# Block 0's attention chain in hand order, its heads four at a time

## The chip, the cores and the metric

The kernel runs on one core of a Trainium2 chip. The metric is device time in microseconds. The engines named below are PE (TensorE, matmuls and transposes), DVE (VectorE), ACT (ScalarE), POOL (GpSimd, which here issues the gathers) and SP (SyncE, which issues most loads). Lines such as L262 are lines of the kernel before; the order listings of the change have lines of the changed file, some 5 to 100 higher.

## The reference, cut

A decoder layer over 512 tokens of width 1024, float32: an attention layer with two groups of eight heads of 64, one output projection, a normalization, then a retrieval layer over 16384 single-neuron experts, and a second normalization.

```python
def hybrid_mixer(x, w_in, w_out):
    proj = x @ w_in                       # six groups of 512 columns
    qa, ka, va, qb, kb, vb = jnp.split(proj, cuts, axis=-1)
    qa = partial_rotary(split_heads(qa, DIL_HEADS), pos)
    ka = partial_rotary(split_heads(ka, DIL_HEADS), pos)
    oa = dilated_window_attention(qa, ka, split_heads(va, DIL_HEADS))
    ob = stick_breaking_attention(...)
    return concatenate([oa, ob]) @ w_out

x = layer_norm(ALPHA * x + mix)
# peer: scores of x @ w_query against sub_keys, top 16 of each half,
# 16 of the sums, softmax gates, then for 128 chosen experts per token
#   h = x . u[e];  y = sum gate * gelu(h) * v[e]
x = layer_norm(ALPHA * x + peer(x))
```

A heads are softmax attention with a mask that holds logarithms of multiplicities; B heads weigh by exponentials of sums of log-sigmoid terms, which the kernel makes with a triangular matmul.

## The kernel before

The 512 tokens are four blocks of 128. Block 0 goes alone and first, in plain float32 (a matmul of two records on PE): its six projection groups, its A heads, its B heads, output projection, normalization, queries of the retrieval, routing. Only then is it known which experts its tokens want, and POOL can start to gather rows of `peer_u` (L739, 128 rows of 4 KB each). Everything for blocks 1 to 3 (projection in split form with three matmuls a product, `mm3`, L127 to L129; A heads; B heads) is laid beside the gathers of blocks 0 and 1. Blocks 2 and 3 go through all experts in dense form later.

The steps of block 0:

- `project_block0` (L244) yields 24 times, four weight loads of 512 KB per group, into four buffers in turn (`WBUF` = 4), each freed by its matmuls (L262). The groups follow `GROUPS` (L225): keys A, values A, queries A, keys B, values B, queries B. `place_tok` (L234) scales the result on ACT (L239), rotates it on DVE (L214 to L217, "rot" groups), and `turn` (L219) transposes it on PE (L222) and copies it on ACT (L223).
- `head_a` (L311) and `head_b` (L334) do one head each. A: scores (L315), mask and minimum on DVE (L318), exponential with sum on ACT (L321), transpose (L325), copy (L328), values (L331). B: scores and mask (L339, L341), three ACT operations (L345 to L347), one on DVE (L349), the triangular matmul (L351), an exponential (L355), values (L359). `close_a`, `close_b` (L362, L368) finish eight heads; `place` (L390) transposes them into `o0f`.
- `project_first` (L467): output projection by column halves, c = 0 over all eight slices of weight rows, then c = 1; `add_out` (L455) adds the residual and takes statistics.
- `normalize` (L503), with its transposes on PE (L173) and copies on ACT (L527) back into `x0f`; then `query_first` (L558) with its matmuls at L568 and L572.
- `load_x2` (L720) loads the four 512 KB blocks of x. `project_in` (L269) is the projection of blocks 1 to 3: in its first group it also loads eight pieces `xt` of 192 KB and splits them on ACT (L207) and DVE (L208); its weights are split at L120 and L124.

Up to here the steps are given as generators, taken in turns (`run`, with a ratio for each), and a scheduler orders the instructions of each engine from them. From the B heads of blocks 1 to 3 on (`tc.manual_schedule`, L929) the order is as written. Each engine and each DMA queue works in its order; SP's queue is one of them.

```python
    run(pb, attend_a(0), load_x2(), (3, 2, 1))
    run(attend_b(0))
    run(project_first())
    norm = normalize(0)
    next(norm)
    run(head(proj, 3))
    run(norm)
    first = query_first()
```

Of the kernel before, what the change touches and what calls it, by code (L numbers as in the profile page):

```python
# [92 lines left out]
def build(ctx, nc, tc, a):  # L93
# [131 lines left out]
    GROUPS = ("rot", kA, 1.0), ("tok", 0, 1.0), ("rot", qA, -0.125), ("t", kB, 1.0), ("tok", 512, 1.0), ("t", qB, 0.125)  # L225
# [7 lines left out]

    def place_tok(tb, kind, dst, scale, ps):  # L234
        if kind == "tok":
            nc.scalar.activation(v[:, tb, dst:dst + 512], ps, AF.Copy)
            return
        q = qw.tile([P, NH, HD], F32, name="q", bufs=2)
        nc.scalar.activation(q.rearrange("p h d -> p (h d)"), ps, AF.Copy, scale=scale)  # L239
        if kind == "rot":  # L240
            rotary(q, tb)
        turn(q, dst)

    def project_block0():  # L244
        for g, (kind, _, scale) in enumerate(GROUPS):
# [3 lines left out]
            for i in range(4):  # L249
# [3 lines left out]
                if g == i == 0:  # L253
                    for k in range(2):
                        (nc.scalar, nc.sync)[k].dma_start(w[:, k], src[:, k])
                        (nc.sync, nc.scalar)[k].dma_start(x0f[:, 2 * k:2 * k + 2], a["xT"][:, 2 * k:2 * k + 2, :P])
                    nc.scalar.dma_start(x0f[:, 4:], a["xT"][:, 4:, :P])
                else:
                    nc.sync.dma_start(w, src)
                for k in range(kn):  # L260
                    kk = kn * kq + k
                    nc.tensor.matmul(ps[:, ch * wd:(ch + 1) * wd], x0f[:, kk], w[:, k], start=kk == 0, stop=kk == KD - 1)  # L262
                yield
# [3 lines left out]
            place_tok(0, kind, dst, scale, ps)  # L267

    def project_in():  # L269
        tbs = PARTS[1]  # L270
        n = len(tbs)
        for g, (kind, _, scale) in enumerate(GROUPS):
# [3 lines left out]
            for i in range(4):  # L276
# [6 lines left out]
                wh, wl = wload(a["w_in"][g, i].rearrange("p (k c) -> p k c", k=kn), [P, kn, wd])  # L283
                if kind == "t" and kq == 0:
# [120 lines left out]
    def attend_a(tb):  # L405
        done = []
        yield from heads_a(tb, done)
        place(done)

    def attend_b(tb):  # L410
        done = []
        yield from heads_b(tb, done)
        place(done)
# [53 lines left out]
    def project_first():  # L467
        for c in range(2):
            ps = bank("h")
            for kq in range(4):  # L470
                w = wraw(a["w_out"][c, kq], [P, 2, 512])
                for k in range(2):
                    kk = 2 * kq + k
                    nc.tensor.matmul(ps, o0f[:, kk], w[:, k], start=kk == 0, stop=kk == KD - 1)
                yield
            add_out(0, c, ps)
# [301 lines left out]
    run(head(pb, 12))  # L778
# [102 lines left out]

    tags = cycle("ab")
    proj = project_in()
# [360 lines left out]
```

## Time and profile before

| what | value |
|---|---|
| median of three runs | 1484.0 us (1479.2, 1484.0, 1486.96) |
| the profiled execution, its own time | 1485.58 us |
| its span, first to last instruction | 1483.7 us |
| granted TensorE clock, mean | 0.966 |
| PE busy, share of the span | 1383.8 us, 93% |
| DVE busy | 1197.7 us, 81% |
| ACT, POOL busy | 520.2 and 694.6 us |
| mean HBM rate | 334 GB/s |

The shares are means over stages with different limits. PE's busy time counts pipelined matmuls from issue to a modelled end. In the chain of work that ended last the gathers of `peer_v` and `peer_u` hold 27% of the span.

### The profile page before, as it was taken

Reading aid. Unit: us, or ns where it says so; the run is one execution under the profiler, and the core shown is the slowest. Engines: PE = TensorE matmul, PEld = TensorE weight load, DVE = VectorE, ACT = ScalarE, POOL = GpSimd, SP = SyncE. Lnnn points to the kernel's source line nnn. Section 1 sums busy time; section 2 is a strip of 40 time slices with the busy share of each in tenths; the row PEclk is TensorE's granted clock in tenths of the full one; section 3 lists DMA queues with packets and bytes.
Section 4 is the critical chain, followed back from the end, with each engine's and each line's share of the span. In section 5 each row is a group of like instructions: output and inputs, shape, how many; then the busy total and the mean of one; then the engine's idle time right before and its main releaser. Section 6 shows DMA issues by size and latency. Waiting matters only on the chain.

```text
span 1483.7 us, 19664 instructions
## 1 busy us (share of the span) xinstructions
PE 1383.8 (93%) x6654; PEld 1119.6 (75%) x6654; DVE 1197.7 (81%) x2473; ACT 520.2 (35%) x1073; POOL 694.6 (47%) x526
## 2 busy tenths in 40 slices
PE   7989889999989999588899999999999999999796
PEld 3659677677648998467678888888888888887575
DVE  0137998878888999999998778778788887888887
ACT  1422334455432111399942222222222222222352
POOL 0000478667755333203556666655556555556200
PEclk9889999999889999799999999999999999999898
DMA  8756899889969999658999999999999999999872
GB/s 290 238 175 219 285 363 330 315 319 391 323 240 401 329 310 310 223 179 285 282 357 410 410 410 409 410 409 410 409 410 410 409 409 410 409 409 405 322 248 89
DMA packets 163221, 495.95 MB, mean 334 GB/s; under 512 B 15376, under 2 KB 48288, under 8 KB 163120
## 3 DMA queue, kind: packets, MB, share of 16 engines
q0 software_dynamic: 74304, 270.13, 48.3%
q1 hardware_dynamic: 86432, 218.66, 40.2%
q10 hardware_dynamic: 2384, 5.90, 1.1%
q8 instruction: 53, 0.87, 0.2%
q14 instruction: 48, 0.39, 0.1%
HBM read 477.78 MB, written 16.84 MB: 333 GB/s over the span
## 4 chain that ended last, share of the span: by engine, by line
PE 35%; DMA 31%; DVE 23%; issue 6%; ACT 4%; POOL 1%; SPq 0%; ACTq 0%; DVEq 0%; POOLq 0%
DMA g<-peer_v,eidx 15%; DMA g<-peer_u,eidx 12%; PE y L1112 8%; PE h L856 7%; DVE x L759 3%; DVE yg L759 3%; DVE o L813 2%; PE m L262 2%; DMA v<-peer_v 2%; PE m L497 1%; POOL g L739 1%; PE tr L497 1%; PE h L359 1%; PE h L331 1%; ACT o L822 1%
## 5 line engine op out<-in xcount | busy, mean ns | idle before, releaser
L739 POOL DMA_INDIRECT g<-peer_u,eidx x256 | 356.5, 1392 | 337.9 <-DVE topi L544 146.3
L739 POOL DMA_INDIRECT g<-peer_v,eidx x256 | 332.3, 1298 | 350.2 <-DVE x L759 112.0
L856 PE MATMUL h<-xf,w 128*128 128x256 f32 x2048 | 474.0, 380 | 0.0
L856 PEld LDWEIGHTS h<-xf,w 128*128 128x128 f32 x2048 | 384.0, 191 | 52.3
L748 DVE SCALAR_TENSOR_TENSOR g<-g,x 128x1024 f32<-128x1024 f32 x256 | 305.5, 1221 | 46.2 <-DMA g<-peer_u,eidx 45.6
L1112 PE MATMUL y<-vh,a 128*128 128x512 f32 x928 | 288.7, 415 | 9.1 <-ACT a L1098 8.3
L1112 PEld LDWEIGHTS y<-vh,a 128*128 128x128 f32 x928 | 175.7, 190 | 50.1 <-ACT a L1098 10.9
L124 DVE TENSOR_TENSOR vl<-v,vh 128x1024 fp32r<-128x1024 f32 x122 | 148.9, 1221 | 44.9 <-ACT vh L1067 44.6
L759 DVE SCALAR_TENSOR_TENSOR x<-g,hg,x 128x1024 f32<-128x1024 f32 x128 | 163.8, 1280 | 23.4 <-DMA g<-peer_v,eidx 22.6
L759 DVE SCALAR_TENSOR_TENSOR yg<-g,hg,yg 128x1024 f32<-128x1024 f32 x126 | 161.4, 1281 | 25.7 <-DMA g<-peer_v,eidx 25.1
L848 ACT ACTIVATE gl<-h 128x256 f32<-128x256 f32 x128 | 48.7, 380 | 310.1 <-PE h L856 310.0
L1112 PE MATMUL y<-vl,a 128*128 128x512 f32 x464 | 147.2, 399 | 1.0 <-DVE vl L124 1.0
L1067 ACT ACTIVATE vh<-v 128x1024 fp32r<-128x1024 f32 x122 | 128.5, 1053 | 38.0 <-PE y L1112 16.2
L1112 PEld LDWEIGHTS y<-vl,a 128*128 128x128 f32 x464 | 87.8, 190 | 22.4 <-DVE vl L124 2.4
L1098 ACT ACTIVATE a<-gl 128x512 fp32r<-128x512 f32 x58 | 36.3, 627 | 167.0 <-DVE gl L1092 167.0
L822 ACT ACTIVATE o<-o1b,sg 128x128 f32<-128x128 bf16 x256 | 83.5, 400 | 3.4 <-DVE o1b L807 3.2
L262 PE MATMUL m<-w,x0f 128*128 128x256 f32 (+1 forms) x128 | 48.6, 523 | 8.6 <-DMA x0f<-xT 7.9
L828 PEld LDWEIGHTS m<-o,o 128*128 128x128 f32 x304 | 37.7, 191 | 20.9 <-ACT o L822 18.0
L828 PE MATMUL m<-o,o 128*128 128x128 f32 x304 | 41.7, 280 | 11.8 <-ACT o L822 7.1
L128 PE MATMUL m<-wl,x2h 128*128 128x512 f32 x96 | 40.3, 420 | 6.1 <-DVE wl L124 6.0
L813 DVE TENSOR_TENSOR o<-sg,c_small 128x512 f32<-128x512 f32 x64 | 43.9, 686 | 2.4 <-PE a L828 2.2
L262 PEld LDWEIGHTS m<-w,x0f 128*128 128x128 f32 x128 | 24.2, 201 | 26.0 <-issue 11.4
(256 smaller groups left out, 1865.2 us busy)
## 6 DMA issues: line engine op xcount, KB each, us to landing
w<-uT SPq DMA_DIRECT2D x128, 512.0 KB, 8.7
v<-peer_v SPq DMA_DIRECT2D x128, 512.0 KB, 7.3
w<-w_in SPq DMA_DIRECT2D x47, 512.0 KB, 5.0
gt<-gd SPq DMA_DIRECT2D x15, 960.0 KB, 11.3
w<-peer_wq SPq DMA_DIRECT2D x16, 512.0 KB, 4.3
wq<-peer_wq SPq DMA_DIRECT2D x16, 512.0 KB, 6.7
gd<-stage SPq DMA_DIRECT2D x15, 512.0 KB, 5.1
gd<-stage SPq DMA_DIRECT2D x15, 448.0 KB, 3.7
```

What stands on the lines that cost most here:

```text
L124: nc.vector.tensor_sub(parts[1], src, parts[0].bitcast(F32))
L262: nc.tensor.matmul(ps[:, ch * wd:(ch + 1) * wd], x0f[:, kk], w[:, k], start=kk == 0, stop=kk == KD - 1)
L739: nc.gpsimd.indirect_dma_start(out=u, out_offset=None, in_=a["peer_v" if kind else "peer_u"], in_offset=bass.IndirectOffsetOnAxis(ap=eidx[ ...
L748: nc.vector.scalar_tensor_tensor(u, u, 1.0, x, op0=OP.mult, op1=OP.mult, accum_out=hs[:, j:j + 1])
L759: nc.vector.scalar_tensor_tensor(acc, u, hs[:, j:j + 1], acc, op0=OP.mult, op1=OP.add)
L813: nc.vector.tensor_tensor(hot2[s], gate[tb][1][:, 0, t:t + TG, None].to_broadcast([P, TG, P]), iota[:, None, :].to_broadcast([P, TG, P]), ...
L822: nc.scalar.activation(hot[s][:, j], o1b[:, :, j], AF.Copy, scale=gate[tb][1][:, 1, t + j:t + j + 1])
L828: nc.tensor.matmul(gps[s][:, j * P:(j + 1) * P], o2[:, j], o1[:, j], start=True, stop=True)
L848: nc.scalar.activation(gls[c // 2][:, c % 2], ps[:, :ND], AF.Gelu)
L856: nc.tensor.matmul(hps[c][:, :ND], us[c][:, k], xf[:, k], start=k == 0, stop=k == KD - 1)
L1067: nc.scalar.activation(vsp[c][0], vs[c], AF.Copy)
L1112: nc.tensor.matmul(yps[t][hf], s_, w_[:, hf * 512:(hf + 1) * 512], start=c == 0 and n == 0, stop=c == P - 1 and n == len(terms) - 1)
```

## The change

It puts block 0's part, from the first 12 projection steps to the second half of normalization, into manual order, and changes how the work is cut:

- The first rows of x come as an array of their own, `x0T`, contiguous, all but one piece through SP's queue.
- Queries B are projected ahead of values B, in block 0 and in blocks 1 to 3. The turn of a group is put off by one or two projection steps (`late`).
- `four_a` and `four_b` take four heads (the even ones, or the odd) as one piece of 512 columns: one score bank, one DVE and ACT operation for each step. In `four_a` the minimum and the sum are separate DVE operations.
- `first_out(kq)` does the output projection by weight rows: slices 0 and 1 for both column halves while only the A half of `o0f` is there.
- x is loaded later; of the eight `xt` pieces two are loaded ahead of the queries instead of eight, and two projection steps of blocks 1 to 3 run there instead of three.

```diff
-    GROUPS = ("rot", kA, 1.0), ("tok", 0, 1.0), ("rot", qA, -0.125), ("t", kB, 1.0), ("tok", 512, 1.0), ("t", qB, 0.125)
+    GROUPS = ("rot", kA, 1.0), ("tok", 0, 1.0), ("rot", qA, -0.125), ("t", kB, 1.0), ("t", qB, 0.125), ("tok", 512, 1.0)
...
-                        (nc.sync, nc.scalar)[k].dma_start(x0f[:, 2 * k:2 * k + 2], a["xT"][:, 2 * k:2 * k + 2, :P])
-                    nc.scalar.dma_start(x0f[:, 4:], a["xT"][:, 4:, :P])
+                        (nc.sync, nc.scalar)[k].dma_start(x0f[:, 2 * k:2 * k + 2], a["x0T"][:, 2 * k:2 * k + 2])
+                    nc.sync.dma_start(x0f[:, 4:], a["x0T"][:, 4:])
...
+                n += 1
+                if n in late:
+                    turn(*late.pop(n))
                 yield
...
-            place_tok(0, kind, dst, scale, ps)
+            if kind == "tok":
+                place_tok(0, kind, dst, scale, ps)
+            else:
+                late[n + (2 if kind == "rot" else 1)] = scaled(0, kind, scale, ps), dst
...
                 wh, wl = wload(a["w_in"][g, i].rearrange("p (k c) -> p k c", k=kn), [P, kn, wd])
+                if g == i == 0:
+                    yield
...
+    def four_a(g, st, tag):
+        ps = bank(tag).rearrange("p (i t) -> p i t", i=4)
+        hs = slice(g, NH, 2)
+        rows = slice(g * 64, g * 64 + 64)
+        for i in range(4):
+            nc.tensor.matmul(ps[:, i], qA[0][rows, i], kA[rows, i, :P], start=True, stop=True)
+        yield
+        u, w = (work.tile([P, 512], F32, name="su", bufs=5).rearrange("p (i t) -> p i t", i=4) for _ in range(2))
+        nc.vector.tensor_add(u, ps, maska[:, None, 3 * P:].to_broadcast([P, 4, P]))
+        nc.vector.tensor_reduce(st["nm"][:, hs], u, axis=AX.X, op=OP.min)
+        nc.vector.tensor_sub(u, u, st["nm"][:, hs, None].to_broadcast([P, 4, P]))
+        nc.scalar.activation(u, u, AF.Exp, scale=-1.0)
+        nc.vector.reduce_sum(st["z"][:, hs], u, axis=AX.X)
+        yield
+        for i in range(4):
+            nc.tensor.transpose(ps[:, i], u[:, i], ident)
+        yield
+        nc.scalar.activation(w, ps, AF.Copy)
+        yield
+        for i in range(4):
+            h = 2 * i + g
+            nc.tensor.matmul(st["po"][:, h * HD:(h + 1) * HD], w[:, i], v[:, 0, h * HD:(h + 1) * HD], start=True, stop=True)
+        yield
+
+    def four_b(g, st, tag):
+        zf = bank(tag)
+        ps = zf.rearrange("p (i t) -> p i t", i=4)
+        rows = slice(g * 64, g * 64 + 64)
+        for i in range(4):
+            nc.tensor.matmul(ps[:, i], kB[rows, i, :P], qB[0][rows, i], start=i == 0, stop=False, skip_group_check=True)
+        for i in range(4):
+            nc.tensor.matmul(ps[:, i], identb, maskb, start=False, stop=False, skip_group_check=True)
+        yield
+        u = work.tile([P, 512], F32, name="su", bufs=5)
+        nc.scalar.activation(u, zf, AF.Abs)
+        nc.scalar.activation(u, u, AF.Exp, scale=-1.0)
+        nc.scalar.activation(u, u, AF.Ln, bias=ones)
+        nc.vector.scalar_tensor_tensor(u, zf, 0.0, u, op0=OP.max, op1=OP.add)
+        yield
+        nc.tensor.matmul(zf, tri, u, start=False, stop=True, skip_group_check=True)
+        nc.scalar.activation(u, zf, AF.Exp)
+        yield
+        for i in range(4):
+            h = 2 * i + g
+            nc.tensor.matmul(st["po"][:, h * HD:(h + 1) * HD], u[:, i * P:(i + 1) * P], v[:, 0, 512 + h * HD:512 + (h + 1) * HD], start=True, stop=True)
+        yield
...
-    def project_first():
+    def first_out(kq):
         for c in range(2):
-            ps = bank("h")
-            for kq in range(4):
-                w = wraw(a["w_out"][c, kq], [P, 2, 512])
-                for k in range(2):
-                    kk = 2 * kq + k
-                    nc.tensor.matmul(ps, o0f[:, kk], w[:, k], start=kk == 0, stop=kk == KD - 1)
-                yield
-            add_out(0, c, ps)
+            if c not in psf:
+                psf[c] = bank(("h", "mm")[c])
+            w = wraw(a["w_out"][c, kq], [P, 2, 512])
+            for k in range(2):
+                kk = 2 * kq + k
+                nc.tensor.matmul(psf[c], o0f[:, kk], w[:, k], start=kk == 0, stop=kk == KD - 1)
+            if kq == 3:
+                add_out(0, c, psf[c])
+            yield
+
+    psf = {}
...
     pb = project_block0()
-    run(head(pb, 12))
+    with tc.manual_schedule():
+        run(head(pb, 12))
...
+    proj = project_in()
+    xload = load_x2()
+    with tc.manual_schedule():
+        def go(steps, n=1):
+            run(head(steps, n))
+
+        st = group(0)
+        a0, a1 = (four_a(g, st, "ab"[g]) for g in range(2))
+        go(pb, 2)
+        go(a0)
+        go(a1)
+        go(a0)
+        go(a1)
+        go(pb, 2)
+        go(a0)
+        go(pb)
+        go(a0)
+        go(a1)
+        go(pb)
+        go(a0)
+        go(a1)
+        go(pb)
+        go(a1)
+        go(pb)
+        place([(close_a(st), 0, 0)])
+        go(xload)
+        go(pb, 2)
+        st = group(0)
+        b0, b1 = (four_b(g, st, "ab"[g]) for g in range(2))
+        go(b0)
+        go(b1)
+        go(b0)
+        go(b1)
+        run(pb)
+        pf = chain(*(first_out(kq) for kq in range(4)))
+        go(b0)
+        go(pf)
+        go(b1)
+        go(pf)
+        go(b0)
+        go(b1)
+        o = close_b(st)
+        next(proj)
+        go(pf, 2)
+        run(xload)
+        place([(o, 0, 4)])
+        run(pf)
+        norm = normalize(0)
+        next(norm)
+        go(proj, 2)
+        run(norm)
     tags = cycle("ab")
-    proj = project_in()
-    run(pb, attend_a(0), load_x2(), (3, 2, 1))
-    tags = cycle(("a", "b", "mm", "mm", "mm"))
-    run(attend_b(0))
-    run(project_first())
-    tags = cycle("ab")
-    norm = normalize(0)
-    next(norm)
-    run(head(proj, 3))
-    run(norm)
...
+        "x0T": x[:P].T.reshape(KD, P, P).transpose(1, 0, 2),
```

What this does to the queues stands in three places. The first is PE at the end of block 0's projections of keys B, where the A heads come in; `m_...` is a projection bank, `a` and `b` are the two score banks, `h` the bank of results. Before:

```order
L222 MATMUL tr<-c_ident,q 128x128 x4
L262 MATMUL m_224<-w,x0f 128x256 x8
L315 MATMUL a<-kA,qA_179 128x128
L315 MATMUL b<-kA,qA_179 128x128
L262 MATMUL m_224<-w,x0f 128x256 x2
L325 MATMUL a<-c_ident,su 128x128
L262 MATMUL m_224<-w,x0f 128x256
L331 MATMUL h<-v,su 128x64
L325 MATMUL b<-c_ident,su 128x128
```

With the change:

```order
L267 MATMUL m_227<-w,x0f 128x256 x8
L222 MATMUL tr<-c_ident,q 128x128 x4
L423 MATMUL a<-kA,qA_181 128x128 x4
L423 MATMUL b<-kA,qA_181 128x128 x4
L267 MATMUL m_227<-w,x0f 128x256 x8
L433 MATMUL a<-c_ident,su 128x128 x4
L267 MATMUL m_289<-w,x0f 128x256 x4
L222 MATMUL tr<-c_ident,q 128x128 x4
L433 MATMUL b<-c_ident,su 128x128 x4
L267 MATMUL m_289<-w,x0f 128x256 x4
L439 MATMUL h<-v,su 128x64 x4
```

All eight heads' scores now stand together, right behind the turn of the queries, and four projection steps stand between the scores and the first values. Before, two heads at a time went through all their steps.

The second place is PE in the B heads' second half (`m_416` to `m_471` are banks of B heads before, `m_411` is the second output bank of the change). Before:

```order
L474 MATMUL h<-w,o0f 128x512
L351 MATMUL m_416<-su,c_tri 128x128
L474 MATMUL h<-w,o0f 128x512
L359 MATMUL h<-v,su 128x64
L351 MATMUL m_427<-su,c_tri 128x128
L351 MATMUL m_438<-su,c_tri 128x128
L351 MATMUL a<-su,c_tri 128x128
L339 MATMUL m_471<-qB_313,kB 128x128
L359 MATMUL h<-v,su 128x64 x3
```

With the change:

```order
L267 MATMUL m_346<-w,x0f 128x512 x4
L457 MATMUL a<-su,c_tri 128x512
L524 MATMUL h<-w,o0f 128x512 x2
L457 MATMUL b<-su,c_tri 128x512
L524 MATMUL m_411<-w,o0f 128x512 x2
L462 MATMUL h<-v,su 128x64 x8
L524 MATMUL h<-w,o0f 128x512 x2
L524 MATMUL m_411<-w,o0f 128x512 x2
L173 MATMUL tr<-c_ident,o 128x128 x4
L524 MATMUL h<-w,o0f 128x512 x2
```

The B scores now stand ahead of the last projection matmuls (`m_346`, values B), and half of the output projection stands ahead of the transposes of B's result; before, four of its sixteen matmuls did.

The third place is SP's queue from the last projection weights to the norm's weights. Before:

```order
L259 DMA w<-w_in 128x1024
L281 DMA xt<-xT 128x384
L259 DMA w<-w_in 128x1024
L464 DMA w<-w_out 128x1024
L549 DMA skT<-skT 128x256 x2
L464 DMA w<-w_out 128x1024
L281 DMA xt<-xT 128x384
L464 DMA w<-w_out 128x1024 x2
L281 DMA xt<-xT 128x384 x2
L464 DMA w<-w_out 128x1024
L281 DMA xt<-xT 128x384
L464 DMA w<-w_out 128x1024 x3
```

With the change:

```order
L264 DMA w<-w_in 128x1024 x4
L514 DMA w<-w_out 128x1024 x2
L292 DMA xt<-xT 128x384 x2
L133 DMA w<-w_in 128x1024
L514 DMA w<-w_out 128x1024 x2
L775 DMA x_100<-x 128x1024 x3
L514 DMA w<-w_out 128x1024 x4
L561 DMA w<-ln_g 128x1024
L561 DMA w<-ln_b 128x1024
L514 DMA w<-peer_wq 128x1024 x2
L292 DMA xt<-xT 128x384 x2
L514 DMA w<-peer_wq 128x1024 x2
```

Three of the four blocks of x, the first weight tile of blocks 1 to 3 (L133) and two `xt` pieces now stand among the output weights; the other six `xt` pieces stand among the query weights. In blocks 1 to 3 the order of the scheduler's part changes with the groups: queries B come ahead of values B, so the last projection group, behind which the B heads start, is now that of the values.

More of the change, by code (lines that the diff above doesn't have):

```diff
@@ L232, in target, with scaled @@
         return dst if isinstance(dst, int) else dst[:, :, SPAN[pair]]
+    def scaled(tb, kind, scale, ps):
+        q = qw.tile([P, NH, HD], F32, name="q", bufs=2)
+        nc.scalar.activation(q.rearrange("p h d -> p (h d)"), ps, AF.Copy, scale=scale)
+        if kind == "rot":
+            rotary(q, tb)
+        return q
     def place_tok(tb, kind, dst, scale, ps):
@@ L237, in place_tok @@
             return
[L238 to L242, printed above, removed]
+        turn(scaled(tb, kind, scale, ps), dst)
     def project_block0():
+        late = {}
+        n = 0
         for g, (kind, _, scale) in enumerate(GROUPS):
@@ L403, in epilogue @@
         yield
[L405 to L413, printed above, removed]
+    def four_a(g, st, tag):
[21 more added lines that the diff above has]
+        yield
@@ L1217, in layout @@
         "xT": x.T.reshape(KD, P, S).transpose(1, 0, 2),
-        "w_in": np.stack([by_tile(f["w_in"].reshape(D, 6, 512)[:, g], g) for g in (1, 2, 0, 4, 5, 3)]),
+        "x0T": x[:P].T.reshape(KD, P, P).transpose(1, 0, 2),
+        "w_in": np.stack([by_tile(f["w_in"].reshape(D, 6, 512)[:, g], g) for g in (1, 2, 0, 4, 3, 5)]),
         "w_out": f["w_out"].reshape(4, 2, P, 2, 512).transpose(3, 0, 2, 1, 4),
```

## The prediction

> **What bounds the kernel now.** I read the busy time by stretches of 20 us first, to see where block 0's chain stands and which resource idles in it; then the chain of work that ended last, in that stretch; then each engine's timeline there; and last the stretches behind it, to see whether time won in front arrives at the end. Columns of the first fence: the stretch in us, its length, busy us of PE, PE's weight loads, DVE, ACT, POOL with counts, the granted clock, the DMA share, GB/s.
>
> ```profile
> 0.00:20.00 20.00, 12.06 (x19) 4.67 (x20) 1.13 (x7) 1.88 (x2) 3.54 (x10) 0.91 0.82 293
> 40.00:60.00 20.00, 19.16 (x83) 11.49 (x83) 3.77 (x16) 7.74 (x25) 0.00 (x0) 1.00 0.89 286
> 60.00:80.00 20.00, 18.62 (x69) 12.60 (x68) 4.26 (x14) 9.39 (x34) 0.00 (x0) 0.66 0.31 106
> 100.00:120.00 20.00, 18.86 (x106) 16.09 (x107) 8.36 (x30) 4.95 (x11) 0.00 (x0) 0.83 0.55 174
> ...
> 112.00:132.00 20.00, 20.00 (x163) 18.58 (x162) 12.47 (x68) 4.71 (x17) 0.00 (x0) 1.00 0.65 219
> 180.00:220.00 40.00, 35.12 (x167) 29.19 (x166) 38.10 (x74) 15.36 (x23) 28.23 (x21) 0.95 0.98 355
> 260.00:305.00 45.00, 44.36 (x242) 32.30 (x241) 35.81 (x69) 20.95 (x43) 28.53 (x22) 1.00 0.88 310
> 1100.00:1300.00 200.00, 200.00 (x902) 170.03 (x901) 163.16 (x169) 52.90 (x83) 114.98 (x85) 1.00 1.03 410
> ```
>
> Up to 60 us PE and the weight stream run together. From 60 to 80 the DMA share falls to 0.31 and the clock to 0.66: the chain of attention steps has neither a transfer nor a full clock. From 180 us on something is always nearly full (DVE 38.10 of 40, then PE 44.36 of 45, then DMA). So block 0 is a serial preface: what shortens it moves all that follows, which is in fixed order and carries no other clock. The rows of the preface:
>
> ```profile
> 1.76 11.87 DMA x0f<-xT
> ...
> 65.59 0.48 PE a L339 x2
> ...
> 85.01 0.60 ACT o L370
> ...
> 86.32 8.70 PE h L474 x20
> 95.03 4.96 DMA w<-w_in
> 100.02 1.06 ACT wh L120
> 101.13 1.65 PE m L127 x3
> ...
> 110.38 0.44 PE tr L173 x4
> 111.25 0.24 PE m L127
> 111.51 0.60 PE h L568 x3
> ...
> 150.95 1.00 POOL L739 DMA_INDIRECT g<-peer_u,eidx  x1 [146.32 <-DVE topi L544]
> ```
>
> The reader sees three waits: for the last piece of x0f, for the B heads one after the other (65.6 to 85.0), and, behind the output projection, a detour over a weight load and its split before the queries start at 111.5. The queries lead to POOL's first gather at 150.95.
>
> **The change, step by step.** The sum goes against the profiled execution's 1485.58 us (span 1483.7, 1.9 around it; 1.6 above the median of the three runs).
>
> *The start.*
>
> ```profile
> 4.36 5.73 PE L262 MATMUL m<-w,x0f 128*128 128x512 f32 x8 [4.36 <-DMA x0f<-xT]
> 13.67 7.11 PE L262 MATMUL m<-w,x0f 128*128 128x512 f32 x12 [3.59 <-DMA x0f<-xT]
> ...
> 21.19 7.03 PE L262 MATMUL m<-w,x0f 128*128 128x512 f32 x16
> ...
> 19.11 0.60 ACT L239 ACTIVATE q<-m 128x512 f32<-128x512 f32 x1 [17.07 <-PE m L262]
> ...
> w<-w_in SPq DMA_DIRECT2D x5, 512.0 KB, 8.3
> ```
>
> PE does four matmuls by 10.1, idles 3.59 for x0f and then runs partly at half clock. Two records are one matmul, so 7.03 us for 16 is 0.88 each. The new input has contiguous rows, and its last piece stands third in SP's queue, ahead of three weight tiles and without the two loads of x. If it lands by 10, the other four end at 10.1 + 3.5 = 13.6, against 18.9 (19.11 less a hop): **5.3 gained**, 0 if it lands as late as before. A rule of the Trainium skill speaks against this part: "DMA: Bandwidth & Descriptors", section "Issuing engines are not separate DMA queues", says that the issuing engine saves only issue time, since all run on the same 16 engines. By it alone the move to SP's queue gives nothing and the end is 1470.6 instead of 1465.3. The trace does not bear it out here: this 256 KB piece took 11.87 us from ACT's queue, while SP's 512 KB loads of the first 16 us took 8.3 (median).
>
> *Projections, A heads and B scores.* Five more groups of 7.03 are 35.2. Four heads at a time are priced by rows of the same shapes, four matmuls each, from later blocks:
>
> ```profile
> 310.70 1.08 PE a L339 x8
> ...
> 322.96 0.91 PE b L351 x2
> ...
> 325.17 0.84 PE h L359 x8
> ...
> 61.98 0.37 PE L315 MATMUL a<-kA,qA 64*128 64x128 f32 x1
> ...
> 304.43 0.69 DVE L365 TENSOR_TENSOR o<-h,rz 128x512 f32<-128x512 f32 x1 [1.50 <-PE h L331]
> ```
>
> Per four: scores 1.08, transposes 0.44, values 0.84. A costs PE 2 x 2.4 and 0.4 for placing, B's scores 2 x 1.5 with four masks at the pace of a transpose (0.11), the four turns of 0.44 another 1.8: 10. On DVE an A group is four operations of 512 columns, two from PSUM, at about 0.69 or less, with one exponential of 0.60 between them: 3.6 per group, in order. Projections hide that, with two exceptions: the first scores stand right behind the turn of A's queries (a copy of 0.60 with hops, 0.9), and the copy of kB stands on ACT behind the second group's exponential (0.5 to 1.1). So the last projection ends at 13.6 + 35.2 + 10 + 1.7 = 60.5, against 61.98 now (the L315 that follows it); but now all of A's close and B stand behind it, and in the change only B's second half does. The B chain on ACT (3 x 0.60) and DVE (0.69) lies under the last four matmuls, 3.5. If that cover fails, 2 us show.
>
> *From there to the end of the output projection.* Two tri matmuls 1.8, 16 matmuls of 0.88 = 14.1, values 1.7, transposes 0.4: 18.0. Two waits are added: the copy of o before the third pair of weight rows (0.75), and one weight buffer that holds the first projection tile of the other blocks, freed only when ACT and DVE have split it (1.06 + 1.23); behind it on SP stand the last three w_out loads, for which PE waits about 1.2. End: 60.5 + 20 = 80.5, against 97.06 now. Two banks instead of one take c = 0 and c = 1 at once: no cost, the second was idle. **15 us more than the 1.5 above.**
>
> *Normalization.*
>
> ```profile
> 97.06 0.69 DVE L457 SCALAR_TENSOR_TENSOR x<-x,h 128x512 f32<-128x512 f32 x1 [4.89 <-PE h L474]
> 98.82 1.41 DVE L514 SCALAR_TENSOR_TENSOR x<-x,mv,w 128x512 f32<-128x512 f32 x2
> 101.11 1.23 DVE L124 TENSOR_TENSOR wl<-w,wh 128x1024 fp32r<-128x1024 f32 x1 [0.88 <-ACT wh L120]
> 104.04 1.41 DVE L519 SCALAR_TENSOR_TENSOR x<-x,lw,w 128x512 f32<-128x512 f32 x2
> 110.22 0.60 PE L173 MATMUL tr<-c_ident,x 128*128 128x128 f32 x4
> ```
>
> Now 97.06 to 111.51 is 14.4. Both splits leave the chain, and PE has 18 matmuls of 0.24 (4.3) queued ahead of the transposes instead of 28, the most of them at half clock. Left are 1.76 to the statistics, 1.41, four small operations (0.75), 1.41, and 1.3 from transposes to queries: 6.7. Queries start at 87.2, against 111.5: 24.3 in all.
>
> *What is given back.*
>
> ```profile
> L208 DVE TENSOR_TENSOR x2l<-xt,x2h 128x384 fp32r<-128x384 f32 x8 | 4.5, 558 | 7.9 <-ACT x2h L207 7.7
> L207 ACT ACTIVATE x2h<-xt 128x384 fp32r<-128x384 f32 x8 | 4.2, 520 | 8.0 <-DMA xt<-xT 8.0
> ...
> PE m L128 <- DVE wl L124: 6.0, 2, 4.7
> DVE g L748 <- DMA g<-peer_u,eidx: 5.3, 5, 1.9
> PE m L129 <- DVE wl L124: 4.8, 1, 4.8
> ```
>
> Two of eight xt pieces are loaded ahead of the queries, before all eight. The other six, 192 KB each, now run among the query weights, and their splits (0.52 on ACT, 0.56 on DVE) among the query copies; ACT's second normalization copy and later copies stand behind splits that wait for xt. PE is 20.00 of 20 busy there, so a stalled copy shows. Bounds 0 (DVE has 12.47 of 20) and 6.5 (all twelve splits); I take 2, nearer the idle. One projection step of nine matmuls (2.1) and one split (1.23) go behind the queries into a stage that is nearly full: 0 to 3.3, I take 2. The A heads of the other blocks and the last two projection groups change places there, at equal work; its price has no row, so -5 to +8 by the two longest waits of PE for a split there (4.7 and 4.8), and I take 0, since PE's total is the same.
>
> Sum: 24.3 - 2 - 2 = 20.3, so 1485.6 - 20.3 = 1465.3; **1465**.
>
> **Rivals.**
>
> *The start is not gained.* x0f and the weights still land as before (DMA share 0.82 in the first row): 5.3 less, 1470.6. Against it: the two loads of x leave the stretch. 0.13. This is the page's rule above as a mechanism.
>
> *The clock falls again.* If 0.66 over 60 to 80 means full and half clock, 13.6 us of it were half, though PE was busy 18.62 of 20; 0.83 over 100 to 120 gives another 6.8. If both recur, half of 20.4 is lost, 10: 1475. Against it: projections or output weights now stand between the small steps. 0.10. The Trainium skill, "TensorE: Matmul & The Clock Gate", "Part 4: PE-mode transpose", says that transposes do not count as busy time for the gate; the row of 60 to 80 agrees, and by it the transposes between normalization and queries would not keep the clock up.
>
> *The middle stage eats part.* Two waits for a split of 4.8 more than now: 1475. 0.08.
>
> *The middle stage gains.* No stall of the given-back kind and 5 from the new order: 1456. 0.12.
>
> *Slower.* One mechanism, in the middle stage: in the change, the last four weight splits on DVE have 11 uses of gathers between them, and 69 matmuls of the last value group, 0.24 each, stand on PE behind the last A head, where 36 of the query group stand now. A use waits for its gather, the split for the use, PE for the split. POOL's longest gather with its issue gap is 1.98 + 0.30:
>
> ```profile
> 196.13 1.98 POOL L739 DMA_INDIRECT g<-peer_u,eidx  x1 [0.30 <-issue]
> ```
>
> If PE stood still for all 11, that is 25, and the longer tail adds up to 33 x 0.24 = 8 if nothing ahead of it gets shorter: 1465 + 33 = 1498. It decides from some nine such waits on (20 us). Against it: DVE waits for gathers five times in that stage today, 5.3 in all. 0.04.
>
> **How the numbers follow.** Forecast 1465 (1459 to 1471): 0.53. The rest as given. A measurement of this kernel tells 0.5%, 7.4 us, from no change. Faster takes the forecast, the start, the better middle and more than half of the two at 1475: 0.88; same 0.09; slower 0.03. The range reaches from the better middle, with its unknown bound (1454), to the two at 1475 and a little beyond: 1454 to 1477.
>
> **What would show it.** The first query matmul near 87 and the first gather near 128 to 130 say that the preface did what I say; the first q copy at 14, the last projection at 61, the last output matmul at 81 say which step missed. PEclk of 1.00 from 20 to 90 rules out the second rival. If the first gather is 20 us earlier and the first B block of the other blocks (310.63 now) is not, the middle stage ate it. I would be wrong if DVE or POOL wait in the middle stage more than today, or if PE stands for the weight buffer much longer than 1.2 us.

## The result, and the profile after

The changed kernel took **1464.4 us** (median of 4 runs, 1463.3 to 1464.9) against 1483.6 in the same job: a ratio of 0.9866, 95% interval 0.9838 to 0.9893. Run again later beside other kernels it took 1466.1, 0.9845 (0.9810 to 0.9880). Its profiled execution took 1464.93, with a span of 1463.2; that is 20.65 us below the profiled execution of before.

The stretches by 20 us of the changed kernel come first (columns as in the prediction), then one stretch from the start to the first gather.

```profile
0.00:20.00 20.00, 14.74 (x32) 6.15 (x33) 1.72 (x9) 2.48 (x3) 3.54 (x10) 1.00 0.87 303
...
60.00:80.00 20.00, 17.95 (x54) 8.94 (x53) 2.25 (x3) 4.75 (x8) 0.00 (x0) 0.91 0.80 296
...
0.00:128.39 128.39, 115.88 (x585) 80.61 (x585) 52.96 (x228) 32.78 (x74) 3.54 (x11) 0.99 0.80 268
```

The same stretch of the kernel before, up to its first gather:

```profile
0.00:150.95 150.95, 134.44 (x615) 90.17 (x615) 52.42 (x243) 39.78 (x118) 3.54 (x11) 0.92 0.68 229
```

From 60 to 80 us the DMA share went from 0.31 to 0.80 and the clock from 0.66 to 0.91. Of the 22.56 us by which the first gather comes earlier, PE's busy time gives 18.56 (134.44 to 115.88) and its idle time 4.00. Much of the busy part is clock: 134.44 us at a mean of 0.92 hold some 10.8 that a full clock would not need, 115.88 at 0.99 some 1.2 (an estimate that takes the mean of the stretch for the busy time).

The places that the prediction named, in the timelines of PE, ACT and POOL of the changed kernel (start, duration, engine, line, operation; in brackets the idle time before it and what ended it):

```profile
14.67 0.60 ACT L236 ACTIVATE q<-m 128x512 f32<-128x512 f32 x1 [12.64 <-PE m L267]
...
59.87 1.02 PE L457 MATMUL a<-su,c_tri 128*128 128x512 f32 x2
...
72.89 2.97 PE L524 MATMUL h<-w,o0f 128*128 128x512 f32 x4 [2.05 <-DMA w<-w_out]
75.65 2.61 PE L524 MATMUL m<-w,o0f 128*128 128x512 f32 x4
...
79.81 1.88 PE L524 MATMUL m<-w,o0f 128*128 128x512 f32 x4
...
87.91 0.52 ACT L207 ACTIVATE x2h<-xt 128x384 fp32r<-128x384 f32 x1 [3.87 <-DMA xt<-xT]
88.34 0.58 ACT L580 ACTIVATE x0f<-tr 128x512 f32<-128x512 f32 x1
...
88.97 2.50 PE L621 MATMUL h<-x0f,w 128*128 128x128 f32 x20 [1.27 <-ACT x0f L580]
...
128.39 1.00 POOL L792 DMA_INDIRECT g<-peer_u,eidx  x1 [123.76 <-DVE topi L597]
```

The block's chain ends where it should, with three things to explain: PE waits 2.05 for w_out and then runs four matmuls (eight records) slowly, ACT's first normalization copy stands behind a split that waits for xt, and the gain of 22.56 at the first gather has shrunk to 19.5 at gather 160 (444.90 against 464.42).

### The profile page after: what moved, and what is told of

Same layout as the page of the kernel before. It is cut to its first block, busy times and chain, and to the rows that moved or that the text cites. A ratio compares the mean times of both kernels' runs of the same rounds, so it can differ in the third digit from the quotient of the medians.

```text
span 1463.2 us, 19573 instructions
## 1 busy us (share of the span) xinstructions
PE 1364.4 (93%) x6642; PEld 1110.5 (76%) x6642; DVE 1198.9 (82%) x2459; ACT 514.4 (35%) x1029; POOL 689.6 (47%) x526
## 4 chain that ended last, share of the span: by engine, by line
PE 37%; DMA 26%; DVE 25%; issue 7%; ACT 4%; POOL 2%; SPq 0%; DVEq 0%; POOLq 0%; ACTq 0%
DMA g<-peer_v,eidx 15%; PE y L1207 9%; PE h L910 9%; DMA g<-peer_u,eidx 8%; DVE x L812 3%; DVE yg L812 3%; PE m L267 2%; POOL g L792 2%; DVE o L867 2%; PE m L550 2%; PE tr L550 1%; ACT o L876 1%; DVE vl L124 1%; DMA v<-peer_v 1%; DVE g L801 1%
## 5 line engine op out<-in xcount | busy, mean ns | idle before, releaser
L792 POOL DMA_INDIRECT g<-peer_u,eidx x256 | 349.4, 1365 | 325.5 <-DVE topi L597 123.8
L267 PE MATMUL m<-w,x0f 128*128 128x256 f32 (+1 forms) x128 | 45.5, 505 | 5.3 <-DMA w<-w_in 5.1
L1186 DVE TENSOR_TENSOR gl<-gl,gt 128x480 f32<-128x480 f32 x64 | 41.8, 652 | 0.0
```

What stands on the lines that cost most here:

```text
L792: nc.gpsimd.indirect_dma_start(out=u, out_offset=None, in_=a["peer_v" if kind else "peer_u"], in_offset=bass.IndirectOffsetOnAxis(ap=eidx[ ...
```

## The experiments

All times are medians; the ratio is to the kernel before in the same job. That kernel's median was 1483.6, 1486.0, 1484.6 and 1489.4 in the four jobs, so medians from different jobs compare to a few us only. "Gather 48 to 128" is the time between the issues of these two gathers, the part of the middle stage in which the projections of blocks 1 to 3 end and their B heads begin.

| kernel | us | ratio (95%) | first gather | gather 48 to 128 |
|---|---|---|---|---|
| before | 1483.6 | | 150.95 | 148.61 |
| changed | 1464.4 | 0.9866 (0.9838 to 0.9893) | 128.39 | 150.59 |
| changed, again | 1466.1 | 0.9845 (0.9810 to 0.9880) | 128.76 | 155.67 |
| start alone | 1478.5 | 0.9947 (0.9923 to 0.9971) | 142.63 | 146.94 |
| last piece on ACT's queue | 1462.2 | 0.9843 (0.9809 to 0.9877) | 126.51 | 152.65 |
| short rows, SP's queue | 1463.2 | 0.9847 (0.9814 to 0.9880) | 126.43 | 152.49 |
| 7 us of matmuls added | 1475.5 | 0.9898 (0.9859 to 0.9937) | 132.70 | 156.44 |
| scheduler's order | 1463.8 | 0.9836 (0.9791 to 0.9881) | 125.44 | 155.94 |
| output by column halves | 1467.9 | 0.9870 (0.9825 to 0.9916) | 131.64 | 157.70 |
| old groups, blocks 1 to 3 | 1458.2 | 0.9802 (0.9760 to 0.9844) | 126.72 | 147.64 |
| the same, again | 1458.2 | 0.9794 (0.9760 to 0.9829) | 126.12 | 147.72 |
| weights of 1 to 3 late | 1468.0 | 0.9869 (0.9812 to 0.9927) | 128.86 | 157.68 |
| heads one at a time | 1473.5 | 0.9910 (0.9874 to 0.9945) | 134.54 | 156.38 |
| scheduler's order, old groups | 1459.5 | 0.9805 (0.9767 to 0.9843) | 124.86 | 147.83 |

### The start: queue or rows

The first run takes the start alone, on top of the kernel before:

```diff
-    (nc.sync, nc.scalar)[k].dma_start(x0f[:, 2 * k:2 * k + 2], a["xT"][:, 2 * k:2 * k + 2, :P])
-nc.scalar.dma_start(x0f[:, 4:], a["xT"][:, 4:, :P])
+    (nc.sync, nc.scalar)[k].dma_start(x0f[:, 2 * k:2 * k + 2], a["x0T"][:, 2 * k:2 * k + 2])
+nc.sync.dma_start(x0f[:, 4:], a["x0T"][:, 4:])
```

> The kernel before with the start of the change alone: x0f is read from the array of its own, its last piece on SP's queue; everything else of block 0 stays in the old order. If a cut at the front of one serial chain goes through to the end, the first query copy comes 4.4 us earlier (as 14.67 against 19.11 in the two traces), the first gather about 4.4 us earlier than 150.95, and the time is near 1479, about 0.3% below the kernel before. Rival: what comes behind the first group waits for the weight stream anyway; then the first copy moves by 4.4, the first score matmuls by under 1, and the time not at all (1483 to 1486).

The first copy of q came at 14.86 (before 19.11), the first gather 8.32 earlier, the time fell by 0.53% (7.9 us). So a cut at the front goes through, and here it gained more than its 4.25 on the way to the first gather. The next two take one half of that edit back from the changed kernel:

```diff
-nc.sync.dma_start(x0f[:, 4:], a["x0T"][:, 4:])
+nc.scalar.dma_start(x0f[:, 4:], a["x0T"][:, 4:])
```

> The changed kernel with the last piece of x0f back on ACT's queue, still read from the array of its own. If the queue made that piece late (11.87 us on ACT's queue before, 4.9 on SP's after), the first query copy goes back to between 17 and 19 and the time rises by 3 to 4.5, to 1468 to 1469. Rival, the long rows did it: the first copy stays at 14.7 within 0.5, and the time at 1464 to 1465.

```diff
-nc.sync.dma_start(x0f[:, 4:], a["x0T"][:, 4:])
+nc.sync.dma_start(x0f[:, 4:], a["xT"][:, 4:, :P])
```

(and the two smaller pieces from xT likewise)

> The changed kernel with x0f cut out of xT again (rows of 512 bytes), in the changed kernel's order of queues, last piece on SP's. If the length of the rows made the piece late, the first query copy goes back to between 17 and 19 and the time to 1468 to 1469. Rival, the queue did it: the first copy stays at 14.7 within 0.5, the time at 1464 to 1465. If both count, this run and the one with the piece on ACT's queue each give back a part, 1.5 to 3 us.

Both theories missed: either half is enough, and neither run gave back the 1.5 to 3 us of the third. The first copy came at 14.48 and 14.97, the times were those of the changed kernel. The DMA view has the piece's way (queue, KB, us from issue to landing); before, then the changed kernel, then the two halves, one fence each:

```profile
x0f<-xT ACTq DMA_DIRECT2D x1, 256.0 KB, 11.9
```

```profile
x0f<-x0T SPq DMA_DIRECT2D x1, 256.0 KB, 4.9
```

```profile
x0f<-x0T ACTq DMA_DIRECT2D x1, 256.0 KB, 7.2
```

```profile
x0f<-xT SPq DMA_DIRECT2D x1, 256.0 KB, 5.8
```

Long rows on ACT's queue cost 2.3, short rows ahead of SP's weight loads 0.9, short rows on ACT's queue in the kernel before 7.0. At 7.2 the piece still lands by 9, before PE has done its first four matmuls, so it does not show in the time. The kernel before differs in one thing more: its two loads of x, 1 MB, are issued at 4.33, while the piece is under way, and no run has short rows on ACT's queue without them. So which of the three made 11.9 of it stays open. With the start alone one of these loads is still there, at 4.45, and the piece, with long rows and on SP's queue, took 5.0.

### How far a delay goes

```diff
         run(norm)
+        ps = bank("h")
+        for k in range(8):
+            nc.tensor.matmul(ps, x0f[:, k], x2[:, 0, :512], start=k == 0, stop=k == 7)
```

> The changed kernel with eight more float32 matmuls of 512 columns on PE just ahead of block 0's queries, whose result nothing reads: 8 x 0.87 = 7.0 us of added work. If block 0 is one chain that sets the end, all of it goes through: first gather 7.0 later than 128.39, time 1471 to 1472. If the middle stage has slack that takes up a late start, as it gave back about 2.7 of an early one: the gather 7.0 later, but the end only 4 to 5 later, 1468 to 1469. Rival, the middle does not depend on when block 0 ends: 1464 to 1465.

The matmuls took 7.13, the first gather moved by 6.2 against the two runs before it in the table (4.3 against the changed kernel's own profile), and the time rose by 9.4 to 11.1 against the changed kernel's two medians and by 12.3 to 13.2 against the two runs before it, which are of the same job. By the ratios it is some 8 (0.9898 against 0.9843 and 0.9847), with the interval of this run's ratio from 2 to 14. So a rise of nothing, which the end of block 0 would give if it did not matter, is unlikely. Slack of 2 or 3 us cannot be excluded; but nothing points to it, since of all middle stages this one was the longest (326.4 us from the first gather to gather 160, against 316.5 in the changed kernel's first profile). For the same reason a part of the rise may be the middle stage's own.

### Cut, order, output projection

The same edits of the computation, but the scheduler orders both stretches:

```diff
-    with tc.manual_schedule():
+    if True:
```

> The changed kernel with the same cut (four heads at a time, row-wise output projection, its own x0 array), but the scheduler free to order the two stretches instead of the order of the code. If the written order carries a large part of block 0's gain, the last projection matmul of block 0 ends 3 to 10 us later than 59.9, the queries start as much later than 85.6 to 89, and the time is 1468 to 1475. Rival, the cut alone does it and the scheduler finds an order as good: queries start within 1.5 of the changed kernel's, time 1461 to 1466.

The queries start at 86.02, the first gather at 125.44, earlier than with the written order (128.39; 126.4 in the two runs with half of the start taken back): the rival holds. **Fixing the written order buys nothing**; what gains is the cut, with the interleaving in which the code hands the steps to the scheduler, which this run keeps.

Its heads are then made one at a time again (`heads_a`, `heads_b` in the mix of before), in the scheduler's order:

```diff
-        a0, a1 = (four_a(g, st, "ab"[g]) for g in range(2))
-        b0, b1 = (four_b(g, st, "ab"[g]) for g in range(2))
+    run(pb, attend_a(0), load_x2(), (3, 2, 1))
+    run(attend_b(0))
+    run(chain(*(first_out(kq) for kq in range(4))))
```

> The changed kernel's start, its order of groups, its delayed turns and its output projection by weight rows, but block 0's heads one at a time as before, in the scheduler's order. It stands against the run that has the four-head cut in the scheduler's order (first gather 125.44, block 0's last projection matmul at 61). If heads four at a time carry most of block 0's gain, the last projection matmul moves to 68 or later, the first gather to 134 to 142, and the time is 1470 to 1478. Rival, the order of the groups, the turns and the output projection carry it: the first gather at 127 to 131, time 1463 to 1468.

Gather and time came as the first theory had them (9.1 later than the run with the four-head cut), but not by its way: the projections ended earlier (57.8), not later. This run also has the loads of x back in the mix. The end of the output projection and what follows, in the PE, ACT and DVE timelines of this run:

```profile
81.74 1.88 PE L524 MATMUL m<-w,o0f 128*128 128x512 f32 x4
...
86.58 1.06 ACT L120 ACTIVATE wh<-w 128x1024 fp32r<-128x1024 f32 x1 [10.14 <-DMA w<-w_in]
...
88.07 1.22 DVE L124 TENSOR_TENSOR wl<-w,wh 128x1024 fp32r<-128x1024 f32 x1
...
93.84 0.60 PE L173 MATMUL tr<-c_ident,x 128*128 128x128 f32 x4
```

and of the run with the cut in the scheduler's order:

```profile
78.04 1.88 PE L524 MATMUL m<-w,o0f 128*128 128x512 f32 x4
...
84.70 0.63 PE L173 MATMUL tr<-c_ident,x 128*128 128x128 f32 x4 [1.42 <-DVE x L572]
```

Only 3.7 of the 9.1 are there when the output projection ends; the other 5.4 arise in the normalization, where the weight tile for blocks 1 to 3 is again loaded last (ACT waits 10.14 for it) and split. The run that moves only that load says what it is worth:

```diff
-        next(proj)
         go(pf, 2)
         run(xload)
         place([(o, 0, 4)])
         run(pf)
+        next(proj)
```

> The changed kernel with the first load of blocks 1 to 3's weights moved behind block 0's output projection, so that it holds none of the weight buffers while w_out streams. If the held buffer makes the wait for w_out (1.4 to 2.0 us at 71 in four traces), that wait goes to under 0.5 and the output projection ends 1.5 to 2 earlier; but the load and its splits then land later, and the first projection matmuls of blocks 1 to 3, which cover the norm of block 0, start late by 1 to 3: time 1461 to 1466. Rival: the wait is the sheer rate of the weight stream (DMA share 0.9 to 1.0 from 66 to 74), then it stays at 1.4 to 2.0 and the time rises by 1 to 3.

From its PE timeline:

```profile
71.55 1.98 PE L524 MATMUL h<-w,o0f 128*128 128x512 f32 x4 [0.69 <-ACT o0f L409]
...
76.81 1.88 PE L524 MATMUL m<-w,o0f 128*128 128x512 f32 x4
...
82.26 0.50 PE L128 MATMUL m<-wl,x2h 128*128 128x512 f32 x1 [2.48 <-DVE wl L124]
...
87.87 0.60 PE L173 MATMUL tr<-c_ident,x 128*128 128x128 f32 x4
```

In the trace both halves of the theory hold. Without the held buffer PE no longer waits for w_out (only 0.69 for o0f) and the output projection ends at 78.7, 1.6 earlier than in the run with short rows; but PE then waits 2.48 for the split, and the normalization's transposes start at 87.87, 2.8 later than there (at 85.06). The early load costs 1.6 and saves 4.4. The time, 1468.0, lay above the forecast range of 1461 to 1466, and its interval does not part it from the changed kernel; the first gather is only 2.4 later than in the run with short rows, and PE's clock from gather 48 to 128 was 0.91 here, against 0.95 there.

Last, the output projection by column halves in the same slots:

```diff
-        pf = chain(*(first_out(kq) for kq in range(4)))
+        pf = chain(*(first_out(c) for c in range(2)))
-        go(pf, 2)
```

> The changed kernel with block 0's output projection by column halves again (four steps for columns 0 to 511, then four for the rest), in the same slots. By weight rows, six of the eight steps read only the first three quarters of o0f and can run ahead of head set B's last piece; by columns the fourth step needs it. If the order by rows buys something, the output projection ends 2 to 4 later than 79.5 to 81.7 and the time is 1465 to 1468; rival: the wait for the weights (1.4 to 2.0 us in every trace so far) hides it, and the end of the projection is the same within 0.7, time 1462 to 1465.

```profile
70.11 5.40 PE L524 MATMUL h<-w,o0f 128*128 128x512 f32 x8 [1.60 <-ACT o0f L409]
75.35 7.03 PE L524 MATMUL m<-w,o0f 128*128 128x512 f32 x16
...
90.79 4.13 PE L621 MATMUL h<-x0f,w 128*128 128x128 f32 x20
```

PE stands for the copy of o (1.60) because the matmuls that used to cover it need that copy now; the projection ends at 82.4, 2.1 later than in the run with short rows, and the first gather is 5.2 later. But PE lost clock in two places here and in none there (stretches of 2 us, the granted clock third from the end):

```profile
72.00:74.00 2.00, 2.00 (x3) 0.68 (x2) 0.55 (x1) 0.00 (x0) 0.00 (x0) 0.50 0.74 244
...
92.00:94.00 2.00, 2.00 (x11) 2.00 (x11) 0.38 (x1) 0.00 (x0) 0.00 (x0) 0.50 0.86 314
```

Eight records at the pace of the sixteen behind them would take 3.5, not 5.40, and the first 20 of the queries took 2.50 there, not 4.13. That is 3.5 of the 5.2, and 1.9 of the 2.1 by which the projection ends later, which is the rival's case. Whether the wait brought the fall of the clock or the fall was a draw is open, so **what the order by rows buys by itself is not shown**. The time, 1467.9, is where the theory had it, with an interval that does not part it from the changed kernel.

### The new order of groups in blocks 1 to 3

```diff
-        for g, (kind, _, scale) in enumerate(GROUPS):
+        for g in (0, 1, 2, 3, 5, 4):
+            kind, _, scale = GROUPS[g]
```

(in `project_in` alone)

> The changed kernel with the old order of groups in blocks 1 to 3 (values of set B ahead of its queries); block 0 keeps the new one. Prediction's step: the swap costs nothing there, time 1462 to 1465, shift of the gathers at block B's start unchanged. Rival: the new order makes B's first score copies queue on ACT behind the copies of v (a wait of 2.31 for su at 297.8 in the changed kernel's trace), and the old order starts B 2 to 3 earlier: 1459 to 1462.

1458.2 is a little below the rival's range, but the changed kernel was not beside it in that job. So it was run again, with that kernel and with the scheduler's order on top:

> The old order of groups in blocks 1 to 3 once more, in more rounds and beside the changed kernel itself. If the new order of groups costs 4 to 6 us in blocks 1 to 3, this run is that much faster than the changed kernel beside it, with intervals that part. If the first one was a draw, the two agree within 3 us.

> The changed kernel itself once more, beside the others on one chip. If a run's middle stage is a draw, its profile differs from the first one of this very kernel by 2 to 10 us between the first gather and gather 160, with a clock there that differs as well, and without a loss of clock at 73 to 77; the median of its time stays at 1462 to 1466. If the middle stage follows from the program, the shifts agree with the first profile within 1 us.

> Two edits together: block 0's stretches in the scheduler's order, and blocks 1 to 3 with the old order of groups. Each alone gave 1463.8 and 1458.2. If the old order of groups is a real gain of 4 to 6 us and the two are independent, the time is 1456 to 1460. If those were draws of the clock in the middle stage (from the first gather to gather 160 the traces of kernels with one and the same middle stage took 314 to 326 us at granted clocks of 0.95 to 0.92), it is the changed kernel's time within 3 us, 1462 to 1466.

The old order gave 1458.2 both times (10 runs, 1453.0 to 1461.5), the changed kernel 1464.4 and 1466.1 (10 runs, 1460.9 to 1473.1): **6 to 8 us**. In the job that has both, the two intervals of the ratio overlap a little, against the expectation, but no run of one kernel reaches into the other's range. Against the two runs with half of the start taken back, whose first gathers come as early as here, and between the two runs in the scheduler's order (1463.8 and 1459.5) it is 4 to 5, in different jobs. The scheduler's order on top adds nothing (1459.5). The column "gather 48 to 128" shows the place: 146.9 to 148.6 in the five traces with the old order, 150.6 to 157.7 in the nine with the new one, with no overlap. From the first gather to gather 160 the two sets do overlap, 313.4 to 318.5 against 314.1 to 326.4, with means 5 us apart. The stretch between gathers 48 and 128 of the changed kernel (its two profiles), then of the old order (second run), then of the kernel before, one fence each:

```profile
229.79:380.38 150.59, 142.92 (x741) 105.85 (x740) 123.80 (x226) 71.08 (x136) 108.60 (x81) 0.97 0.92 331
```

```profile
226.23:381.90 155.67, 145.92 (x739) 107.24 (x739) 123.48 (x226) 71.07 (x136) 106.41 (x80) 0.94 0.89 321
```

```profile
226.33:374.05 147.72, 143.07 (x749) 106.89 (x749) 124.28 (x226) 70.77 (x136) 105.95 (x81) 0.96 0.92 339
```

```profile
251.63:400.24 148.61, 143.66 (x751) 107.32 (x749) 123.00 (x224) 71.01 (x136) 107.68 (x80) 0.97 0.92 337
```

Length less PE's busy time is PE's idle time: 7.67 and 9.75 with the new order, 4.65 and 4.95 with the old one. Over all traces it is 7.6 to 9.8 in the nine and 4.6 to 5.0 in the five. So 2.6 to 5.2 us of idle time come with the new order every time: each of the nine has a wait for a weight split (1.4 to 3.5 in all), which none of the five has. What differs from trace to trace is the busy time, 142.9 to 150.1 in the nine at clocks of 0.97 to 0.91, and 142.0 to 143.7 in the five at 0.97 to 0.96. The DVE and PE timelines in that stretch, first of the changed kernel, run again:

```profile
275.36 2.36 DVE L124 TENSOR_TENSOR wl<-w,wh 128x1024 fp32r<-128x1024 f32 x2
...
284.75 1.23 DVE L801 SCALAR_TENSOR_TENSOR g<-g,x 128x1024 f32<-128x1024 f32 x1 [2.45 <-DMA g<-peer_u,eidx]
285.90 0.08 DVE L801 DVE_READ_ACCUMULATOR g<-g,x 128x1 f32 x1
285.90 1.22 DVE L124 TENSOR_TENSOR wl<-w,wh 128x1024 fp32r<-128x1024 f32 x1
...
287.18 0.50 PE L128 MATMUL m<-wl,x2h 128*128 128x512 f32 x1 [2.09 <-DVE wl L124]
...
296.35 2.08 PE L364 MATMUL a<-su,c_tri 128*128 128x512 f32 x2 [2.31 <-DVE su L362]
```

and its stretch of 10 us behind that:

```profile
300.00:310.00 10.00, 10.00 (x41) 7.05 (x40) 7.34 (x14) 4.14 (x7) 7.87 (x8) 0.70 1.03 414
```

The weight split stands on DVE behind a gather's use, the use waits 2.45 for its gather, and PE waits 2.09 for the split; five uses in a row ahead of an earlier split (it starts at 275.36) had cost PE another 1.43. With 2.31 at the first B head that is 5.8, of which the old order has 1.97 too; and then the clock is at 0.70 from 300 to 310 us. The first profile of that kernel has one wait for a split (1.4), and on ACT at the same place:

```profile
291.00 1.96 ACT L243 ACTIVATE v<-m 128x512 f32<-128x512 f32 x3 [6.02 <-PE m L129]
...
294.68 0.59 ACT L358 ACTIVATE su<-a 128x512 f32<-128x512 f32 x1
```

Three copies of v stand ahead of what the first B head needs. With the old order (second run), the copies of the last group are those of qB (ACT and PE timelines, then the stretch):

```profile
284.10 1.01 ACT L313 ACTIVATE qB<-m 128x384 f32<-128x384 f32 x2 [6.97 <-PE m L129]
287.37 0.59 ACT L359 ACTIVATE su<-a 128x512 f32<-128x512 f32 x1
...
291.55 2.08 PE L365 MATMUL a<-su,c_tri 128*128 128x512 f32 x2 [1.97 <-DVE su L363]
```

```profile
300.00:310.00 10.00, 10.00 (x61) 7.68 (x61) 7.73 (x15) 5.41 (x9) 8.36 (x6) 1.00 1.03 410
```

PE has no wait for a split here. The first triangular matmul of block 1 starts at 291.55, 6.26 earlier than in the first profile (297.81), of which 2.27 was there at the first gather and another 1.2 at gather 48. Its wait for ACT and DVE is only 0.34 shorter than with the copies of v, so the queue on ACT, the rival's reason, is the small part; the splits are the larger. Why the clock falls more often with the new order was not tried.

Of the other expectations, the changed kernel's middle stage was a draw, as its first theory had it (316.5 and 322.4 us from the first gather to gather 160); but the loss of clock at 73 to 77, which that theory took for a single draw, came again.

## Why the prediction came out as it did

The forecast was 1465, the time 1464.4. The mechanism was right, block 0 is a serial preface and what shortens it moves the rest: the first gather came 22.56 earlier, and the first triangular matmul of block 1 came 19.85 earlier (317.66 to 297.81). But two sizes behind the preface were wrong in opposite directions, so that the total came within 1 us is luck.

- *The start.* Predicted 5.3, measured 4.44 (19.11 to 14.67). The piece of 11.87 us was named rightly; that its queue would have to change was not needed. The piece landed by 6.6, earlier than the 10 of the forecast; but PE started 0.26 later than before and waited 0.53 for a weight tile, which the forecast had at nothing. The rule weighed against this part (the Trainium skill, "DMA: Bandwidth & Descriptors", "Issuing engines are not separate DMA queues") would leave the time where it was if the piece changed its queue alone. With long rows that is so, the first copy comes at 14.48 from ACT's queue and at 14.67 from SP's; with short rows the piece took 11.9 from ACT's queue and 5.8 from SP's, in kernels that differ in the loads of x as well, so no run here decides it.
- *Projections and heads.* Predicted end 60.5, measured 59.87: right.
- *Output projection.* Predicted end 80.5, measured 81.69. The wait for the held buffer is there, with 2.05 in place of 1.2, and it was followed by a fall of the clock that other traces of the same code do not have; without it (the run with short rows) the end is 80.28.
- *Normalization to queries.* Predicted 87.2, measured 88.97: the 1.19 from the output projection, and 0.58 more on the way, where PE waits 1.27 for the first copy, which stands behind a split that waits for xt. The prediction had named that stall, but behind the start of the queries.
- *The query stage was to give back 2.* It gave back nothing: 39.44 from queries to first gather before (111.51 to 150.95), 39.42 after. The stall was taken at its entry instead.
- *The moved projection step was to give back up to 3.3, taken as 2.* The three traces of the change with the old order of groups took 97.8 to 101.2 us from the first gather to gather 48 and 147.6 to 147.8 from there to gather 128, the kernel before 100.68 and 148.61. It gave back nothing that can be seen.
- **The step that failed:** "The A heads of the other blocks and the last two projection groups change places there, at equal work; its price has no row, so -5 to +8 ..., and I take 0." The work is equal, but PE waits 2.6 to 5.2 us more and often loses clock: it costs 4 to 8 in the medians. In its first profile only 2.0 of that showed (150.59 against 148.61), the least of nine traces, which is why its span agrees with the sum so well.

So the sum of 20.3 took 24.3 for block 0, where 22.5 came (111.51 to 88.97), took off 4 that were not given back, and took off nothing for the order of the groups. In the first profile 22.5 less 2.0 is 20.5, against 20.65 measured. The medians do not add up as well: 22.5 less 4 to 8 is 14.5 to 18.5, against 19.2 in the first job and 23 by the ratio of the second; with the old order of groups they gain 26 to 31, where the two profiles gain 24 to 25. These few us have no place in the traces and stay open.

The rival that ended slower named the mechanism of that loss, a use that waits for its gather, a split behind the use and PE behind the split; it had 11 such waits for the price of 33, and the traces show one or two, with the clock beside them. The clock did not fall over 60 to 80 as the second rival had it (0.91, and 1.00 from 80 to 120), though 0.50 from 74 to 76 shows that it could. Of the row of 60 to 80 that the rival reads, some 2.4 of 18.62 busy us are transposes, so it says little about them. Those between normalization and queries cost no clock in the changed kernel (1.00 from 80 to 100), but behind them it fell in the run with the output by column halves (0.50 from 92 to 94).

## What to carry to other kernels

When a list of steps is reordered for one stage, look for every other loop that reads the same list: here the new order of groups, which belongs to block 0's chain, cost 4 to 8 us in blocks 1 to 3, and keeping it to block 0 (1458.2) beats both kernels. What it brings in block 0 by itself was not tried. A term that has no row and wide bounds should be tried by itself first, and a total that agrees with the sum does not show that the terms do. Before a stretch is ordered by hand, compare the same cut in the scheduler's order: it was as good (1463.8), because the gain lay in the steps themselves. Two of them the runs price: heads four at a time with the later loads of x, some 3.7 us up to the end of the output projection, and loading early what the next stage splits, some 2.4 at the first gather.

## What the runs showed of the hardware

The same code, in kernels that differ elsewhere, lost clock at one place or did not. In the changed kernel, run again, PE waited for w_out as in other traces, and the clock fell to half (stretches of 2 us; the columns as before, the granted clock third from the end):

```profile
73.64 3.56 PE L524 MATMUL h<-w,o0f 128*128 128x512 f32 x4 [2.74 <-DMA w<-w_out]
```

```profile
72.00:74.00 2.00, 0.36 (x1) 0.31 (x2) 0.00 (x0) 0.00 (x0) 0.00 (x0) 0.96 0.99 379
74.00:76.00 2.00, 2.00 (x3) 0.68 (x2) 0.00 (x0) 0.00 (x0) 0.00 (x0) 0.50 0.77 313
```

In the run with short rows it did not, after a wait of 2.04:

```profile
73.17 1.96 PE L524 MATMUL h<-w,o0f 128*128 128x512 f32 x4 [2.04 <-DMA w<-w_out]
```

```profile
74.00:76.00 2.00, 2.00 (x6) 0.93 (x5) 0.00 (x0) 0.00 (x0) 0.00 (x0) 1.00 0.92 358
```

With 2.05 (changed kernel, first profile) the clock fell, with 2.04 (here), 2.06 (old order, again) and 2.08 (old order) it did not, and behind a wait of 1.60 (output by column halves) it fell as well. So the length of the wait alone does not decide it. The Trainium skill, "TensorE: Matmul & The Clock Gate", "Part 1: The HAM clock gate (the "warmup" mystery)", says that the gate judges PE's activity in free-running windows, so that it depends on where in a window the work falls; the traces agree in that equal waits end differently, and no run here moves a wait against the windows, so the cause stays open. From the first gather to gather 160 the two profiles of the changed kernel took 316.5 and 322.4 us, so a single profile is uncertain there by several us, and a term of 2 us can only be judged over several traces.
